# A row maximum over 64 MB: all loads but the first issued from GpSimd's queue in place of SP's

## The chip, the cores and the metric

The kernel runs on one core of a Trainium2 chip. The time is that of the device, in microseconds (us), for one execution of the whole program. A time called that of the kernel is the median of its runs; a profile is one execution of it, recorded by the hardware profiler, whose own time is given beside its span.

## The reference

```python
def setup_inputs():
    batch, seq, dim = 32, 512, 1024
    return {"x": np.random.randn(batch, seq, dim).astype(np.float32)}

def reference(x):
    return np.max(x, axis=-1).astype(np.float32)
```

There are 32 x 512 = 16384 rows of 1024 float32 values, 67.1 MB in all, and of each row the largest value is wanted: 16384 values, 64 KB. Each value of the input is read once and compared once.

## The kernel before, in words

The 16384 rows are spread over the 128 partitions of the on-chip memory, 128 rows for each partition. "A row" below means one row of 1024 values (4 KB) in every partition, that is 0.5 MB in all; the kernel handles 128 such rows.

The list `BLOCKS` fixes, ahead of time, how many rows each load brings. The first list has 15 loads, of 14, 13, 12, 11, 9, 8, 8, 7, 6, 5, 5, 4, 4, 3 and 3 rows (112 in all); the second has three loads of two rows and nine of one row (15), and then comes one last row that is loaded in two halves (lines 67 and 68). Each partition's rows of one list lie one behind the other in DRAM, so a load of n rows is, for each partition, one unbroken run of n x 4 KB.

The rows land in `ring`, a buffer with room for `RING = 45` rows per partition. A load takes the next free stretch of it, and goes back to its beginning where the stretch would run over the end (lines 54 and 55). So loads 1, 2 and 3 (14 + 13 + 12 = 39 rows) fit side by side; load 4 (11 rows) goes back to row 0, where load 1 lay; load 5 lies over what loads 1 and 2 held, load 6 over loads 2 and 3, loads 7 and 8 over load 3 and beyond, and so on.

One load (line 57) and one reduction on VectorE (line 58) make a step. The reduction reads all n rows of the load and writes n maxima per partition into `res`. The framework puts in the waits: a reduction waits until its load has landed; a load waits until the reductions that read the rows it overwrites are through; and a load also waits for the landing of the load eight before it, since there are eight completion semaphores that take turns. VectorE works in program order, and so does the queue of each engine that issues loads.

All 29 loads are issued from SP (SyncE), on its hardware queue. GpSimd (POOL) does nothing but four small MEMSETs of constants at the start, which the framework adds. TensorE has no work.

At the end, the last row's first half is reduced into the element of `tail` that lies just ahead of the second half (line 69), and the final reduction goes over that element and the second half together (line 70). Two stores are issued from ScalarE: that of the first 112 rows' maxima, held back until the last reduction of the loop (lines 73 and 74), and that of the other 16 (line 75).

Of the kernel before, what the change touches and what calls it, by code (L numbers as in the profile page):

```python
# [1 line left out]

# [4 lines left out]


F32 = mybir.dt.float32

BLOCKS = [
    [14, 13, 12, 11, 9, 8, 8, 7, 6, 5, 5, 4, 4, 3, 3],
    [2, 2, 2, 1, 1, 1, 1, 1, 1, 1, 1, 1],
]
RING = 45
SYNC = mybir.DependencyInfo(mybir.DependencyClass.Sync, mybir.DependencyReason.DATA)


@with_exitstack
def kernel(
    ctx: ExitStack,
    tc: tile.TileContext,
    x: bass.AP,
    out: bass.AP,
):
    nc = tc.nc
    P = 128
    X = mybir.AxisListType.X  # L30

    xf = x.flatten_outer_dims()
    N, D = xf.shape
    H = D // 2
    I = N // P
    of = out.flatten_outer_dims()

    once = ctx.enter_context(tc.tile_pool(name="once", bufs=1))
    ring = once.tile([P, RING, D], F32)
    res = once.tile([P, I], F32)  # L40

    PAD = 16
    tail = once.tile([P, PAD + H], F32)

    at = first = 0
    views = []
    for loads in BLOCKS:
        S = sum(loads) + (loads is BLOCKS[-1])
        xb = xf[first * P:(first + S) * P, :].rearrange("(p i) d -> p i d", p=P)
        dst = bass.AP(tensor=of.tensor, offset=of.offset + first * P, ap=[[S, P], [1, S]])  # L50
        views.append((dst, res[:, first:first + S]))
        b = 0
        for n in loads:
            if at + n > RING:
                at = 0
            xc = ring[:, at:at + n, :]
            nc.sync.dma_start(out=xc, in_=xb[:, b:b + n, :])  # L57
            reduce = nc.vector.reduce_max(out=res[:, first + b:first + b + n], in_=xc, axis=X)  # L58
            at += n
            b += n  # L60
        first += S
    assert first == I

    if at + 1 > RING:
        at = 0
    half = ring[:, at, :H]
    nc.sync.dma_start(out=half, in_=xb[:, b, :H])
    nc.sync.dma_start(out=tail[:, PAD:], in_=xb[:, b, H:])
    nc.vector.reduce_max(out=tail[:, PAD - 1:PAD], in_=half, axis=X)  # L69
    nc.vector.reduce_max(out=res[:, I - 1:], in_=tail[:, PAD - 1:], axis=X)  # L70


    store = nc.scalar.dma_start(out=views[0][0], in_=views[0][1])
    tc.add_manual_dep(store.ins, reduce.ins.name, SYNC, reason="behind the loads")
    nc.scalar.dma_start(out=views[1][0], in_=views[1][1])


# [1 line left out]
_INS = ['x']  # L79
_OUTS = [((32, 512), 'float32')]  # L80


# [23 lines left out]
```

## Time and profile before

| | before |
|---|---|
| median of the runs | 164.97 us (164.94 to 165.01, two runs) |
| the profiled execution | 165.17 us |
| its span, first to last instruction | 163.4 us |
| VectorE busy | 139.0 us, 29 instructions |
| GpSimd busy | 0.2 us, 4 instructions |
| read from DRAM | 67.11 MB, 411 GB/s over the span |
| the SP queue's packets, as a share of 16 DMA engines | 96.6% |

In the profile, DVE is VectorE, POOL is GpSimd, SP is SyncE; SPq is SP's queue with the loads that it issues. L57 is line 57 of the kernel. The page cuts the span into 40 slices and gives, for each, the busy share in tenths (9 is 90% or more). A group of instructions is shown as line, engine, operation, output<-input with their shapes, then the busy time and the mean of one in nanoseconds, and at the end how long the engine had been idle before them and what ended that idle time. A line of DMA issues ends with the size in KB and the time in microseconds from the issue to the landing. The timeline gives start, length, engine, line and operation; in brackets is the idle time before it and what ended it. The waits give engine, line, what was waited for, the total in microseconds, how many times, and the longest. The chain that ended last is followed back from the last instruction, at each step to what released it. A table by stretch of time gives the stretch, its length, VectorE's and GpSimd's busy time with the number of instructions, the granted TensorE clock, the DMA share and the GB/s.

### The profile page before, as it was taken

The page shows a single profiled execution, that of the slowest core. Times are in us where ns is not written, and L with a number is a line of the kernel's source. Part 1 is how long each engine was busy: PE and PEld are TensorE (multiplying, and loading weights), DVE is VectorE, ACT ScalarE, POOL GpSimd, SP SyncE. Part 2 cuts the span into 40 slices and gives each one's busy share as a digit, 9 for nine tenths or more (in the row PEclk, how much of TensorE's full clock was granted, in tenths as well). Part 3 has the DMA queues.
Part 4 walks back from the last instruction along what each step waited for, and adds up shares of the span by engine and source line. Part 5 has one row for each costly group of instructions (what it writes and reads, how often), then busy time and mean ns, then how long its engine had stood idle before and what let it go on. Part 6 is the DMA issues. An engine that isn't in the chain of part 4 may idle for free.

```text
span 163.4 us, 117 instructions
## 1 busy us (share of the span) xinstructions
DVE 139.0 (85%) x29; POOL 0.2 (0%) x4
## 2 busy tenths in 40 slices
DVE  0000099989998999999999999999999999999994
POOL 0000000000000000000000000000000000000000
DMA  6999999999989989999989999999999999999990
GB/s 225 449 449 449 433 417 417 417 401 529 433 385 430 452 386 432 433 433 441 457 385 481 401 442 422 409 438 421 446 409 425 437 410 422 427 407 409 409 355 16
DMA packets 4464, 67.18 MB, mean 411 GB/s; under 512 B 752, under 2 KB 752, under 8 KB 2160
## 3 DMA queue, kind: packets, MB, share of 16 engines
q1 hardware_dynamic: 4176, 67.11, 96.6%
q10 hardware_dynamic: 288, 0.07, 0.2%
HBM read 67.11 MB, written 0.07 MB: 411 GB/s over the span
## 4 chain that ended last, share of the span: by engine, by line
DVE 49%; DMA 48%; SPq 1%; issue 0%
DMA ring<-in_x_dram 48%; DVE res L58 48%; SPq L57 1%; DVE res L70 0%; DVE tail L69 0%
## 5 line engine op out<-in xcount | busy, mean ns | idle before, releaser
L58 DVE TENSOR_REDUCE res<-ring 128x1 f32<-128x1024 f32 (+12 forms) x27 | 137.7, 5165 | 22.1 <-DMA ring<-in_x_dram 22.1
L70 DVE TENSOR_REDUCE res<-tail 128x1 f32<-128x513 f32 x1 | 0.7, 686 | 0.0
L69 DVE TENSOR_REDUCE tail<-ring 128x1 f32<-128x512 f32 x1 | 0.7, 682 | 0.0
L90 POOL MEMSET const-bfloat16-1.0<- 128x1 bf16 x1 | 0.1, 102 | 0.0
L90 POOL MEMSET const-uint8-127<- 128x1 uint8 x1 | 0.1, 102 | 0.0
L90 POOL MEMSET const-float32-0.0<- 128x1 f32 x1 | 0.1, 99 | 0.2 <-issue 0.2
L90 POOL MEMSET const-float32-1.0<- 128x1 f32 x1 | 0.1, 99 | 0.0
## 6 DMA issues: line engine op xcount, KB each, us to landing
ring<-in_x_dram SPq DMA_DIRECT2D x2, 4096.0 KB, 25.6
ring<-in_x_dram SPq DMA_DIRECT2D x1, 7168.0 KB, 19.6
ring<-in_x_dram SPq DMA_DIRECT2D x1, 6656.0 KB, 34.9
ring<-in_x_dram SPq DMA_DIRECT2D x1, 6144.0 KB, 48.9
ring<-in_x_dram SPq DMA_DIRECT2D x1, 5632.0 KB, 28.5
ring<-in_x_dram SPq DMA_DIRECT2D x2, 2560.0 KB, 38.4
ring<-in_x_dram SPq DMA_DIRECT2D x1, 4608.0 KB, 24.7
ring<-in_x_dram SPq DMA_DIRECT2D x9, 512.0 KB, 13.8
```

Of the source, the lines that this page charges most:

```text
L57: nc.sync.dma_start(out=xc, in_=xb[:, b:b + n, :])
L58: reduce = nc.vector.reduce_max(out=res[:, first + b:first + b + n], in_=xc, axis=X)
L69: nc.vector.reduce_max(out=tail[:, PAD - 1:PAD], in_=half, axis=X)
L70: nc.vector.reduce_max(out=res[:, I - 1:], in_=tail[:, PAD - 1:], axis=X)
L90: nc = _bacc.Bacc("TRN2", target_bir_lowering=False, num_devices=1)
```

## The change

Load 1 (14 rows) is issued from SP as before. The other 26 loads of the loop and the two halves of the last row are issued from GpSimd, whose DMAs go through the software queue[...]. The sizes, the order, the ring, the reductions and the stores are the same.

```diff
@@ in the loop over loads
             xc = ring[:, at:at + n, :]
-            nc.sync.dma_start(out=xc, in_=xb[:, b:b + n, :])
+            queue = nc.gpsimd if first + b else nc.sync
+            queue.dma_start(out=xc, in_=xb[:, b:b + n, :])
             reduce = nc.vector.reduce_max(out=res[:, first + b:first + b + n], in_=xc, axis=X)
@@ the last row, in two halves
     half = ring[:, at, :H]
-    nc.sync.dma_start(out=half, in_=xb[:, b, :H])
-    nc.sync.dma_start(out=tail[:, PAD:], in_=xb[:, b, H:])
+    nc.gpsimd.dma_start(out=half, in_=xb[:, b, :H])
+    nc.gpsimd.dma_start(out=tail[:, PAD:], in_=xb[:, b, H:])
```

`first + b` is the number of rows loaded so far; it is zero for load 1 alone.

## The prediction

> **What bounds the kernel now.** I read the page first (parts 1 to 3), then the DMA issues with their landings, then the timeline of the first 64 us, then the waits, and last the chain of waits. From the page, busy time, queues and issues:
>
> ```profile
> DVE 139.0 (85%) x29; POOL 0.2 (0%) x4
> ...
> DVE  0000099989998999999999999999999999999994
> ...
> DMA  6999999999989989999989999999999999999990
> ...
> q1 hardware_dynamic: 4176, 67.11, 96.6%
> ...
> ring<-in_x_dram SPq DMA_DIRECT2D x1, 7168.0 KB, 19.6
> ring<-in_x_dram SPq DMA_DIRECT2D x1, 6656.0 KB, 34.9
> ring<-in_x_dram SPq DMA_DIRECT2D x1, 6144.0 KB, 48.9
> ```
>
> Two resources are nearly full at once. The DMA engines work from start to end (96.6%). VectorE (DVE) is idle for five slices and then full to the end. The 4176 packets of the SP queue are 29 loads of 144, that is 128 data packets (one for each partition's whole run) and 16 completions. So the first load, 14 rows of 4 KB per partition, is 128 packets of 56 KB, eight on each of the 16 engines. The last three lines are loads 1, 2 and 3, with time from issue to landing. The timeline shows how they were issued and what waited for them:
>
> ```profile
> 0.73 1.32 SPq L57 DMA_DIRECT2D ring<-in_x_dram  x3
> 20.31 15.09 DVE L58 TENSOR_REDUCE res<-ring 128x14 f32<-128x14336 f32 x1 [20.31 <-DMA ring<-in_x_dram]
> 35.43 0.33 SPq L57 DMA_DIRECT2D ring<-in_x_dram  x1
> 36.05 14.02 DVE L58 TENSOR_REDUCE res<-ring 128x13 f32<-128x13312 f32 x1 [0.65 <-DMA ring<-in_x_dram]
> 50.58 12.95 DVE L58 TENSOR_REDUCE res<-ring 128x12 f32<-128x12288 f32 x1 [0.51 <-DMA ring<-in_x_dram]
> ...
> 160.38 0.69 DVE L70 TENSOR_REDUCE res<-tail 128x1 f32<-128x513 f32 x1
> ```
>
> Three loads are issued together, within 1.3 us, and they arrive strictly one behind the other: at 20.3, 36.05 and 50.6 us. That is what one queue does: load 1 has all 16 engines to itself. Load 2 (6.816 MB) takes 15.74 us after load 1, or 433 GB/s; this is the full rate that I use below. At it load 1 alone (7.34 MB) is 16.95 us of moving, 2.12 us a packet on each engine, and a packet of load 2 (52 KB) is 15.74/8 = 1.97 us. The waits:
>
> ```profile
> DVE res L58 <- DMA ring<-in_x_dram: 22.1, 5, 20.3
> ...
> SPq L57 <- DVE res L58: 77.4, 7, 15.1
> SPq L57 <- DMA ring<-in_x_dram: 59.4, 13, 18.2
> ```
>
> This is the line that decides. Of VectorE's 22.1 us of waiting, 20.3 are for the very first load; after that only 1.8 us in four waits are left in 140.8 us. VectorE's own work, once begun, is therefore a second bound that lies only 1.8 us below the first. Any delay of the first landing beyond 1.8 us goes to the end of the kernel one for one. The chain of waits gives the same picture from the other side: 48.5% of it is loads and 48.0% reductions on line 58.
>
> **What the Trainium skill says.** (1) The page "DMA: Bandwidth & Descriptors", section "Queues, rings and completion order", says that each DMA engine goes round-robin between the queues that have work for it, a packet of one and then a packet of the next. The trace of before cannot confirm it, since only the SP queue carries loads. (2) The same page, "Issuing engines are not separate DMA queues", says that DMAs of different issuing engines run on the same 16 engines and interleave. (3) Its section "SWDGE vs HWDGE vs iDMA" gives the software queue's packets as preferably at most 4096 B and at most 64 descriptors; for a run of 52 KB that leaves open whether it is one packet or cut. (4) "SBUF — State Buffer", section "Who interferes with whom", says that a tensor reduce on this chip never contends with GpSimd for the SBUF port, so VectorE should not starve the software descriptor generation; nothing in the trace of before shows it.
>
> **The change, part by part.** The bytes, the 29 reductions, the ring of 45 rows and the two stores stay. What moves:
>
> *SP's waits move to POOL.* Twenty-eight issues, with their waits for reductions and for earlier landings, go from SP to POOL. Behind a waiting issue on POOL stand only later loads, as on SP now; POOL's own work is four MEMSETs of 0.1 us before the loads begin. No other engine waits for POOL. Cost of the move itself: nothing, as long as the software issue is hidden.
>
> *The software issue.* The trace of before has no software DMA. A hardware issue takes 0.33 to 0.44 us of SP; the skill gives about 1 us to the first byte for the software path against 0.6 (same DMA page, "Latency and other measured facts"), so per load between nothing and, doubling it for safety, 2 us. I take 1 us. Its cover is worked out below and is over 8 us; only where POOL needs more than about 1.28 us per issue in the run of one-row loads would it eat into that cover, slowly.
>
> *Load 1 stands alone on SP, and loads 2 and 3 start beside it.* This is the part that counts. Neither of loads 2 and 3 waits for anything, so POOL issues them at about 0.8 us, and their packets reach the engines about when load 1's do. By round-robin each engine then takes a packet of load 1, one of load 2, one of load 1. Load 1 has eight packets on each engine; between its first and its eighth stand seven of load 2, 7 x 1.97 = 13.8 us. Load 1 lands at 20.3 + 13.8 = 34.1 us. Load 2 lands two us later, at 36.1, no earlier than now, and VectorE has no use for it before load 1 in any case. Bounds: eight packets in front if POOL comes first (36.0 us); six if POOL's first packet comes some 4 us late or an engine has already taken up a second packet of load 1 (32.1 us). I take seven.
>
> *What VectorE does from there.* It starts at 34.1. Reduction 1 ends at 49.2, reduction 2 at 63.1, reduction 3 at 76.1. Is it ever starved again? Load 4 (11 rows, slots of load 1) is issued at 49.2; load 3 has emptied the engines at about 50.6, load 4 needs 5.77 MB / 433 = 13.3 us plus up to 2 for its start, and lands near 65; it is wanted at 76.1. Load 5 (9 rows, needs load 2's slots) is issued at 63.1, lands near 76, is wanted at 87.9. Loads 6, 7 and 8 need load 3's slots and are issued at 76.1; they land near 88, 98 and 106, wanted at 97, 106 and 115. From there on the engines run without a gap at the old pace and the last half row lands near 163, wanted at 172. So each load is 8 to 11 us early, VectorE works without a pause, and this is the cover that hides the software issues, the two or three DMA gaps of about 1 us after reductions 1 to 3, and a transfer rate up to about 7% lower over the last 113 us.
>
> *Sum.* 34.1 (start) + 139.0 (VectorE busy, page) = 173.1. In the profile of before the span ends 2.3 us after VectorE (163.4 against 160.38 + 0.69), for the last store and the closing waits: 175.4. The profiled execution took 165.17 us for a span of 163.4, 1.77 us around it: 177.2. The profiled execution lies 0.2 us above the median of the runs, 164.97, so **177.0** for a median. Put as a difference: 13.8 us of delay less the 1.8 us of idle time that vanishes, +12.0 us, 7.3%.
>
> **Rivals.**
>
> *R1, not slower: load 1 goes first after all.* If its eight packets are drained as one turn (one DMA is one packet for the arbiter), or if the software queue's first bytes come very late, loads 2 and 3 arrive behind it as now. VectorE starts at 20.3 and the time is 165 to 165.5. For it: load 1 is issued a little earlier than POOL can be heard, and the trace shows no case of two queues. Against: the two statements of the skill on interleaving, and one packet per partition in the page's counts. The point from which it decides: within 2% (3.3 us) the first landing may slip by 3.3 + 1.8 = 5.1 us, two packets of load 2 in front instead of seven; POOL's first byte would have to come later than about 12 us.
>
> *R2, the software queue cuts runs into small packets.* Eight turns of 4 KB cost load 1 almost nothing (8 x 1.97/13 = 1.2 us), but all later loads then move at the rate of short packets. The stretch from 140 to 150 us, where loads have one and two rows, moved 414 GB/s:
>
> ```profile
> 140.00:150.00 10.00, 10.00 (x5) 0.00 (x0) 1.00 1.01 414
> ```
>
> The 59.8 MB behind load 1 then take 144.4 us in place of 138.1, and a last stage 2 to 3% slower still is possible: +6 to +8 us, 171 to 173.
>
> *R3, the software queue keeps its turn for a whole DMA.* Then an engine takes one packet of load 1, all of load 2, one of load 1, all of load 3, and the other six. Load 1 lands when all three have, at 50.6 us; 50.6 + 139.0 + 2.3 + 1.8 = 193.7. Against it: packets preferably small.
>
> **How the numbers follow.** Forecast (5.5 to 8.5 packets in front, or a little end work on POOL) 0.70, own range 174.5 to 179.5; R1 0.13; R2 0.08; R3 0.06; the rest, 0.03, something slower still, or a gain that I see no source for, since VectorE's 139.0 us cannot begin before load 1's 17 us of moving. The range 169 to 181 holds the forecast and R2 and leaves R1 and R3 out, 0.19. A measurement of this kernel tells 2% from no change; faster by that 0.02, within it 0.14, slower 0.84.
>
> **What would show it.** In the page's DMA part a second queue with 28 x 144 = 4032 packets; more if runs are cut (R2). Load 1 from issue to landing about 33 us in place of 19.6, load 2 nearly as it was. VectorE idle for eight slices in place of five, then without a wait. VectorE's waits: one of about 34 us and nothing else. Busy time 139.0 as before. The DMA row with dips after 50, 65 and 76 us and an early end. The forecast is wrong if VectorE starts near 20 us (R1) or near 50 (R3), or if it starts at 34 and waits for loads later, which would mean a slow software path.

## The result, and the profile after

| | before | after |
|---|---|---|
| median of the runs | 164.97 us | 180.09 us (180.09 to 180.10, two runs) |
| ratio to before | | 1.092, 95% interval 1.089 to 1.094 |
| the profiled execution, its span | 165.17 us, 163.4 us | 180.09 us, 178.3 us |

The kernel is 15.1 us slower. From the page of the changed kernel, the lines that answer to those shown of before:

```profile
DVE 138.7 (78%) x29; POOL 15.0 (8%) x32
...
DVE  0000000099999999997999999999999999999994
...
DMA  6999999989870047989989999999999999999980
...
q0 software_dynamic: 3904, 59.77, 78.9%
q1 hardware_dynamic: 144, 7.34, 9.9%
...
ring<-in_x_dram SPq DMA_DIRECT2D x1, 7168.0 KB, 33.2
ring<-in_x_dram POOLq DMA_DIRECT2D x1, 6656.0 KB, 34.6
ring<-in_x_dram POOLq DMA_DIRECT2D x1, 6144.0 KB, 48.5
```

Load 1, 7168 KB, now takes 33.2 us from issue to landing, where it took 19.6. Loads 2 and 3 take what they took (34.9 and 48.9 before), although they come from the software queue, `q0 software_dynamic` on the page. VectorE is idle for eight slices and not five; then it is full, but for one slice with a 7. GpSimd's 15.0 us are, but for the four MEMSETs, the time of its 28 issues. The DMA row has a hole that the forecast did not have, slices 13 to 15. The waits of the changed kernel have this line for VectorE (total, times, longest):

```profile
DVE res L59 <- DMA ring<-in_x_dram: 37.2, 3, 35.9
```

And its timeline, first up to 100 us, of which the first issues are shown, then in stretches from 45 to 62, from 60 to 66 and from 74 to 82 us (PEq is TensorE's sequencer, which has no work here):

```profile
1.25 2.22 POOL L58 DMA_DIRECT2D ring<-in_x_dram  x4 [0.81 <-PEq L102]
3.47 0.54 POOL L69 DMA_DIRECT2D tail<-in_x_dram  x1
...
35.90 29.01 DVE L59 TENSOR_REDUCE res<-ring 128x13 f32<-128x13312 f32 x2 [35.90 <-DMA ring<-in_x_dram]
...
49.84 27.93 DVE L59 TENSOR_REDUCE res<-ring 128x14 f32<-128x14336 f32 x2
65.21 1.05 POOL L58 DMA_DIRECT2D ring<-in_x_dram  x2 [61.20 <-DVE res L59]
...
64.83 15.20 DVE L59 TENSOR_REDUCE res<-ring 128x12 f32<-128x12288 f32 x3
...
81.17 11.89 DVE L59 TENSOR_REDUCE res<-ring 128x11 f32<-128x11264 f32 x1 [1.14 <-DMA ring<-in_x_dram]
```

The first reduction is that of load 2 (13 rows), at 35.9 us; that of load 1 (14 rows) comes second, at 49.84. The compiled program has exchanged the two. It has also brought two one-row reductions forward, behind that of load 3 (the group x3 from 64.83). Their loads and that of the very last half row (L69) go out at the start, behind loads 2 and 3. POOL's next load, number 4, must wait for reduction 1, whose rows it overwrites, and goes out at 65.21 us, 61.2 us after POOL's last issue at the start. So VectorE waits for it once more, 1.14 us.

The sum closes: start 35.9, VectorE busy 138.7, its later waits 37.2 - 35.9 = 1.3, from VectorE's end to the span's end 2.3 (178.3 - 175.34 - 0.69): 178.2 us against the measured 178.3.

The packet records of the trace show what happened to load 1. These are the starts, in us, of the first to the eighth packet on a DMA engine (each time that of the earliest of the 16 engines; the others follow within 0.9 us):

```
before, load 1 (56 KB)   1.72  4.54  6.66  8.77 10.88 13.00 15.11 17.22   last one ends 19.95
after,  load 1 (56 KB)   1.74  4.54  8.62 12.70 16.78 20.85 24.93 29.01   last one ends 31.59
after,  load 2 (52 KB)   6.66 10.74 14.82 18.89 22.97 27.05 31.12 33.09   last one ends 35.52
```

After two packets of load 1 the queues alternate strictly, one packet each, until load 1 is done. Six packets of load 2 stand ahead of its last one. Yet it lands only at 0.74 + 33.2 = 33.9 us, 2.3 us after its last byte, where before it was 0.35. The completion is a packet too, one of 4 bytes on each engine, and it waits for one more packet of load 2 (31.12 to 33.09): the 16 completions of load 1 start from 33.09 to 33.55 us. That makes seven turns in all, the number of the forecast, but six of them ahead of the last data packet and one ahead of the completion.

### The profile page after: what moved, and what is told of

It reads as the page before. It is cut to its first block, busy times and chain, and to the rows that moved or that the text cites. A ratio compares the mean times of both kernels' runs of the same rounds, so it can differ in the third digit from the quotient of the medians.

```text
span 178.3 us, 115 instructions
## 1 busy us (share of the span) xinstructions
DVE 138.7 (78%) x29; POOL 15.0 (8%) x32
## 3 DMA queue, kind: packets, MB, share of 16 engines
q0 software_dynamic: 3904, 59.77, 78.9%
## 4 chain that ended last, share of the span: by engine, by line
DVE 60%; DMA 38%; issue 0%; POOL 0%; PEldq 0%
DVE res L59 59%; DMA ring<-in_x_dram 38%; DVE res L71 0%; DVE tail L70 0%; POOL ring L58 0%; PEldq L102 0%
## 5 line engine op out<-in xcount | busy, mean ns | idle before, releaser
L59 DVE TENSOR_REDUCE res<-ring 128x1 f32<-128x1024 f32 (+12 forms) x27 | 137.5, 5161 | 37.2 <-DMA ring<-in_x_dram 37.2
L58 POOL DMA_DIRECT2D ring<-in_x_dram x26 | 13.8, 533 | 147.7 <-DVE res L59 116.6
L68 POOL DMA_DIRECT2D ring<-in_x_dram x1 | 0.5, 541 | 2.2 <-DVE res L59 2.2
L69 POOL DMA_DIRECT2D tail<-in_x_dram x1 | 0.5, 541 | 0.0
## 6 DMA issues: line engine op xcount, KB each, us to landing
ring<-in_x_dram SPq DMA_DIRECT2D x1, 7168.0 KB, 33.2
```

Source lines behind the costliest of these rows:

```text
L58: queue.dma_start(out=xc, in_=xb[:, b:b + n, :])
L68: nc.gpsimd.dma_start(out=half, in_=xb[:, b, :H])
L69: nc.gpsimd.dma_start(out=tail[:, PAD:], in_=xb[:, b, H:])
```

## The experiments

Two theories stood against each other: A, that the loss comes from two queues that have work at once, at the start; B, that the software queue is slow. And the order of the instructions had to be told apart from both. The diffs below are against the changed kernel, that of the second run against the first. Where the order is held, the ties of the first run are in place too and are not shown again, and the two halves of the last row go by the queue of the late loads.

**The order of the source.** The changed kernel, with each load and each reduction tied to the one before it on its engine; the tie orders the instructions and adds no wait:

```diff
+    def pin(engine, made):
+        if engine in last:
+            tc.add_manual_dep(made.ins, last[engine].ins.name, ORDER, reason="program order")
+        last[engine] = made
+        return made
-            queue.dma_start(out=xc, in_=xb[:, b:b + n, :])
-            reduce = nc.vector.reduce_max(...)
+            pin(queue, queue.dma_start(out=xc, in_=xb[:, b:b + n, :]))
+            reduce = pin(nc.vector, nc.vector.reduce_max(...))
```

> The changed kernel with its loads and its reductions held in the order of the source (14, 13, 12, 11 rows and so on); the queues are those of the change. Theory A (two queues take turns packet by packet, so load 1 lands near 34 us, and the rest of the loss is the order: the compiled change reduces load 2 ahead of load 1 and brings two one-row loads forward): VectorE starts at 34 us with load 1 and never waits again; 177.0 us, about 3 us less than the change. Rival B (the software queue is slow by itself): the order is worth nothing, it stays at 180.

Measured: 176.45 us, 1.070 of before (1.068 to 1.071), 3.6 us less than the change. VectorE's line in the waits:

```profile
DVE res L68 <- DMA ring<-in_x_dram: 33.9, 1, 33.9
```

The timeline up to 100 us:

```profile
33.89 71.92 DVE L68 TENSOR_REDUCE res<-ring 128x14 f32<-128x14336 f32 x6 [33.89 <-DMA ring<-in_x_dram]
49.27 0.53 POOL L67 DMA_DIRECT2D ring<-in_x_dram  x1 [46.82 <-DVE res L68]
```

One wait in the whole kernel, 33.9 us, and load 4 issued at 49.27. This is the forecast's schedule. Its order is that of before, the queues are those of the change, and it still loses 11.5 us.

**Only the loads in order**, with the reductions left to the compiler (which exchanges the first two again, but brings none forward):

```diff
-            reduce = pin(nc.vector, nc.vector.reduce_max(...))
+            reduce = nc.vector.reduce_max(...)
```

> Queues as in the change; only the loads are held in the order of the source, while the reductions keep the order that the compiled change gives to its first ones (load 2 ahead of load 1, then load 3, load 4 and so on, with no one-row reductions brought forward). If the exchange of the first two reductions carries the rest of the loss: VectorE starts near 35.9 us with load 2, reduction 1 ends near 65, load 4 can be issued only then and lands near 81, while reduction 3 ends at 77.8, so VectorE waits some 3.4 us (in the change 2.4 us of that were filled by two one-row reductions): 181.5 to 182.5 us, slower than the change. If the loads brought forward (GpSimd's queue filled with small loads ahead of load 4) carried it: about 176.5 us, as with everything in order.

Measured: 182.36 us, 1.106 of before (1.104 to 1.107). The timeline up to 100 us:

```profile
35.94 41.87 DVE L68 TENSOR_REDUCE res<-ring 128x13 f32<-128x13312 f32 x3 [35.94 <-DMA ring<-in_x_dram]
65.24 1.04 POOL L67 DMA_DIRECT2D ring<-in_x_dram  x2 [62.80 <-DVE res L68]
...
81.27 21.55 DVE L68 TENSOR_REDUCE res<-ring 128x11 f32<-128x11264 f32 x2 [3.46 <-DMA ring<-in_x_dram]
```

That is 5.9 us more than with both held, and the order of the two runs differs in reductions 1 and 2 alone. So it is their exchange that costs, in two ways: VectorE starts 2.0 us later (35.9 against 33.9), and load 1's rows in the ring come free at 65 us and not at 49, which makes load 4 late. The loads and reductions brought forward are a help: they fill 2.3 of the 3.46 us. No run held the reductions alone.

**All loads on the software queue**, order held:

```diff
-            queue = nc.gpsimd if first + b else nc.sync
+            queue = nc.gpsimd
```

> As in the run with the order held, but load 1 too is issued from GpSimd, so only one queue carries loads. A: load 1 lands near 20.8 us (half a microsecond later than from SP, since GpSimd issues it at 1.25 us and not at 0.74), no turns are taken, 165 to 166 us, as before the change. B: at least 180, as every load now goes through software.

Measured: 165.87 us, 1.005 of before (1.004 to 1.007). The page has a single queue for the loads:

```profile
q0 software_dynamic: 4048, 67.11, 96.1%
```

The timeline has the first issues and the first three reductions:

```profile
1.24 1.72 POOL L67 DMA_DIRECT2D ring<-in_x_dram  x3 [0.80 <-PEq L111]
21.16 15.09 DVE L68 TENSOR_REDUCE res<-ring 128x14 f32<-128x14336 f32 x1 [21.16 <-DMA ring<-in_x_dram]
...
36.89 14.02 DVE L68 TENSOR_REDUCE res<-ring 128x13 f32<-128x13312 f32 x1 [0.64 <-DMA ring<-in_x_dram]
...
51.42 12.95 DVE L68 TENSOR_REDUCE res<-ring 128x12 f32<-128x12288 f32 x1 [0.51 <-DMA ring<-in_x_dram]
```

Everything goes through software and the kernel is 0.9 us slower than before. This is the timeline of before, 0.85 us late. B falls here. Of the 0.9 us, 0.5 is that POOL issues at 1.24 us where SP issued at 0.73, and 0.4 that the first packet comes 1.38 us after the issue (at 2.62) and not 0.99 (at 1.72).

**Two hardware queues**, load 1 from SP and the others from ScalarE, order held:

```diff
-            queue = nc.gpsimd if first + b else nc.sync
+            queue = nc.scalar if first + b else nc.sync
```

> Order held, load 1 from SP, all others from ScalarE's hardware queue; no software queue at all. A: hardware queues take the same turns, load 1 lands near 34 us, 176.5 to 177.5 us. B: about 165, as there is no software left.

Measured: 178.52 us, 1.082 of before (1.080 to 1.084). That is outside A's numbers by 1 us, and on the side away from B: there is no software left, and the loss is larger.

```profile
q10 hardware_dynamic: 4320, 59.84, 80.4%
q1 hardware_dynamic: 144, 7.34, 10.0%
```

That is the page; the timeline up to 100 us:

```profile
0.72 99.21 ACTq L67 DMA_DIRECT2D ring<-in_x_dram  x11
0.73 0.37 SPq L67 DMA_DIRECT2D ring<-in_x_dram  x1
35.76 71.92 DVE L68 TENSOR_REDUCE res<-ring 128x14 f32<-128x14336 f32 x6 [35.76 <-DMA ring<-in_x_dram]
```

ScalarE issues at 0.72 us, half a microsecond ahead of POOL, and load 2's first packet starts at 4.48 us in place of 6.49 with the order held: one turn more, eight of 1.97 us, which is 20.3 + 15.7 = 36.0 us against the measured 35.76. The prediction had eight turns as a bound; the expectation for this run left them out.

**Loads 1 to 3 on SP, the rest on the software queue**, order held:

```diff
-            queue = nc.gpsimd if first + b else nc.sync
+            queue = nc.gpsimd if first + b >= 39 else nc.sync
```

> Order held, loads 1, 2 and 3 from SP, loads 4 to 29 from GpSimd's software queue. Load 4 waits for reduction 1, so the two queues barely have work at once. A: load 1 lands near 20.3 us, 165 to 166 us. B: 26 of the 28 moved loads are still software, so most of the loss stays, 178 or more.

Measured: 174.03 us, 1.055 of before (1.053 to 1.057). Both expectations missed. The issues on its page, with the time to landing:

```profile
ring<-in_x_dram SPq DMA_DIRECT2D x1, 7168.0 KB, 19.2
ring<-in_x_dram SPq DMA_DIRECT2D x1, 6656.0 KB, 34.6
ring<-in_x_dram SPq DMA_DIRECT2D x1, 6144.0 KB, 58.6
```

Its timeline, with reductions 1 and 3 and the issue of load 4:

```profile
20.01 15.09 DVE L68 TENSOR_REDUCE res<-ring 128x14 f32<-128x14336 f32 x1 [20.01 <-DMA ring<-in_x_dram]
35.41 0.67 POOL L67 DMA_DIRECT2D ring<-in_x_dram  x1 [34.97 <-DVE res L68]
...
60.26 12.95 DVE L68 TENSOR_REDUCE res<-ring 128x12 f32<-128x12288 f32 x1 [10.50 <-DMA ring<-in_x_dram]
```

Load 1 lands at 20.0 us, as A has it, and the loss comes from A's mechanism at another place, which the expectation overlooked: load 4 is issued at 35.41 us, when load 3 has hardly begun (its first packet starts at 35.01). From the packet records, load 4 comes in after three of load 3's eight packets; the other five and the completion take turns with packets of 44 KB: 6 x 1.67 = 10.0 us. Load 3 lands 9.7 us late (60.24 against 50.5 in before), and the step waits 10.50 us for it.

**Small packets on the other side.** Loads 2 and 3 as two loads of every other row each, so that a packet is one row (4 KB), order held:

```diff
+            if n in (13, 12):
+                for odd in (0, 1):
+                    pin(queue, queue.dma_start(out=xc[:, odd::2, :], in_=xb[:, b + odd:b + n:2, :]))
+            else:
                 pin(queue, queue.dma_start(out=xc, in_=xb[:, b:b + n, :]))
```

> Order held, queues as in the change, but loads 2 and 3 are each issued as two loads of every other row, so that each of their packets is 4 KB and no longer 52 or 48 KB; load 1 keeps its 56 KB packets. Theory A1 (a turn is a packet, whatever its size): between load 1's packets stand seven or eight packets of 4 KB at about 0.16 us each, so load 1 lands near 21.5 us, not 34; loads 2 and 3 move some 6% slower in all, and the time is 166 to 168 us. Rival A2 (the two queues share the bytes evenly): load 1 lands near 34 us as with large packets, 177 us.

**Half the packet size.** Load 2 as one load of 7 rows and one of 6, order held:

```diff
-    [14, 13, 12, 11, ...
+    [14, 7, 6, 12, 11, ...
```

> Order held, queues as in the change, but load 2 of 13 rows is split into one of 7 and one of 6 rows, each with its own reduction. A1 (a turn is a packet): seven packets of 28 KB (1.06 us each) stand in front of load 1's landing, 20.3 + 7.4 = 27.7 us, and the kernel takes 27.7 + 139.2 + 4.1 = 171 us. A2 (even shares of bytes): load 1 lands near 34 us, 177 us.

Measured: 166.92 us (1.011 of before, 1.009 to 1.013) with small packets and 170.27 us (1.032, 1.030 to 1.033) with half. Load 1's issue line in each, small packets first:

```profile
ring<-in_x_dram SPq DMA_DIRECT2D x1, 7168.0 KB, 20.7
```

```profile
ring<-in_x_dram SPq DMA_DIRECT2D x1, 7168.0 KB, 26.9
```

A turn is a packet, whatever its size; the even share of bytes falls. The landing moves with the size of the other queue's packets alone: landed at 21.4 us with 4 KB (0.16 us a packet), 27.7 with 28 KB (1.06 us), 33.9 with 52 KB (1.97 us). Seven turns on 20.3 give 21.4, 27.7 and 34.1. The run with small packets loses 1.9 us and not only these 1.1, because VectorE then waits 0.9 us more for loads 2 and 3 than before.

**Load 2 waits for load 1's landing**, on the software queue, order held:

```diff
+            if first + b == 14:
+                tc.add_manual_dep(load.ins, load1.ins.name, SYNC, reason="load 1 alone")
```

> Order held, queues as in the change, but the first load on GpSimd (load 2) waits until load 1 has landed; so load 1 has the DMA engines to itself and the software queue carries the rest. Theory A: VectorE starts at 20.3 us; load 2's first packet goes out about 1.4 us after load 1 has landed, 21.7 us in place of 19.3, and as the loads bound the kernel this gap of 2.4 us comes out at the end: 167 to 168 us. If the software queue were the cause: 176 or more.

Measured: 168.34 us, 1.020 of before (1.019 to 1.022), 0.3 us above what A gave. The timeline up to 100 us:

```profile
20.31 15.09 DVE L72 TENSOR_REDUCE res<-ring 128x14 f32<-128x14336 f32 x1 [20.31 <-DMA ring<-in_x_dram]
20.59 1.20 POOL L67 DMA_DIRECT2D ring<-in_x_dram  x2 [20.14 <-DMA ring<-in_x_dram]
...
39.40 14.02 DVE L72 TENSOR_REDUCE res<-ring 128x13 f32<-128x13312 f32 x1 [4.01 <-DMA ring<-in_x_dram]
```

Load 1 is back at 20.31 us. Load 2 lands at 39.4 and not at 36.05, and these 3.35 us are the loss of 3.4. Its first packet starts 2.6 us later than in before (21.96 against 19.34), and 2.65 us pass to the start of its second where it is 1.97 between the later ones; this second part was not in the expectation. No version beat the kernel before.

## Why the prediction was right, and where it was off

The measured 180.09 us lie in the range of 169 to 181, but above the 174.5 to 179.5 that the prediction gave for its own case. 11.5 us of the 15.1 come from the mechanism that it forecast, at 12.0. The other 3.6 have a cause that no term of it stood for; that the wide range took them in was luck.

- *What bounds the kernel.* VectorE's 139 us behind load 1's landing, with 1.8 us of room. Right: in all runs in which VectorE waits for load 1 alone, the time is that landing plus 142.6 to 142.8 us (33.9 and 176.45; 35.8 and 178.52; 27.7 and 170.27).
- *Load 1 at 34.1 us by taking turns.* Right, at 33.9, though the count of seven is in part luck. The prediction had all seven ahead of the last data packet; there were six, its lower bound, and the completion, for which it had no turn, added the seventh. The statements of the Trainium skill on turns by packet and on interleaving ("DMA: Bandwidth & Descriptors", "Queues, rings and completion order" and "Issuing engines are not separate DMA queues") are borne out, with one packet of load 1 every 4.08 us in place of every 2.11, and the runs with smaller packets show that it is packets that take turns, not bytes. Why load 2's first packet came only after two of load 1 is open: POOL issued it at 1.25 us, and it started at 6.66, 5.4 us later, where with a single queue it was 1.38.
- *The step that failed: "It starts at 34.1. Reduction 1 ends at 49.2".* The forecast read the order of work from the source, and so do the sections on the kernel and on the change, which calls the order the same. For loads and reductions that don't depend on one another the compiled program need not keep it: reductions 1 and 2 were exchanged once their loads stood in different queues. Against the kernel with the order of the source this cost 3.6 us (180.09 - 176.45). By the trace it is 2.0 us of later start and 1.3 us of waiting later on (35.9, and 1.14 of the 1.3, in the lines of after), and 0.2 us of busy time. The kernel with the order of the source is what the sum of the prediction describes, and lies 0.55 us below its 177.0: 0.2 us of the start and 0.5 of VectorE's busy time, 138.5 us in the three runs with a single wait, less 0.2 by which a profile of before was longer than the median and this one is not. Why the compiler chose this order is open.
- *The software issue is hidden.* Right, and smaller than assumed: 0.53 us per issue, and the first packet comes 1.38 us after it where the hardware queue took 0.99, so 0.4 us more. The packet durations are the same, 1.06 us for 28 KB in either queue.
- *R1 (load 1 first after all) and R3 (a whole DMA as a turn)* fall by the packet records. *R2 (runs cut to 4 KB)* falls too. The count of 3904 packets is not the 4032 that the prediction named: software put the 256 runs of 2 KB of the two half rows into 128 packets of 4 KB, which accounts for the whole difference, and it left longer runs whole, up to the 56 KB of load 1 in the run with all loads in software. For the short runs that agrees with what the Trainium skill gives as the preferred packet, at most 4096 B ("DMA: Bandwidth & Descriptors", "SWDGE vs HWDGE vs iDMA"); the long ones lie far above it.
- *VectorE and GpSimd do not disturb each other.* So it looks here: the 12-row reduction took 12.94 us with two of POOL's issues beside it (65.21 to 66.26) and 12.95 before, the 9-row one 9.74 us with two beside it and without.
- *DMA dips after 50, 65 and 76 us and an early end.* Right for the most part in the order of the source: by the packet records of the run that holds it, the DMA engines stand idle for about 1 us near 50 and near 76 us, hardly near 65, and the loads end near 163. Wrong in the changed kernel, which has one hole from 53 to 66 us while load 4 waits for the exchanged reduction 1. It cost 1.14 us only, since VectorE had work until 80.

## What to carry to other kernels

If one load is awaited ahead of all others, keep everything that could run beside it in the same queue behind it, or make the other queue's packets small: in these runs a second queue took every second turn, and a turn is a packet, here one partition's unbroken run, up to 56 KB and 2.1 us. The delay of the awaited load was, in every such run and within 0.4 us, the number of its packets per DMA engine that were still to come when the other queue's first packet started, and one for its completion, times the other queue's packet time: 6 + 1 in the change, 7 + 1 with ScalarE's queue, 5 + 1 for load 3 in the run with three loads on SP. It counts in full where the consumer has no idle time left; here 1.8 us of idle time took up a part. And look at the compiled order before working out a schedule; moving loads between queues can change the order of instructions that nobody touched.

## What the runs showed of the hardware that was not expected

- The completion of a load takes a turn of its own. From the end of load 1's last data packet to its landing it took 0.35 us with one queue, and 0.55, 1.4 and 2.3 us beside packets of 4, 28 and 52 KB.
- The software queue joins short runs, two of 2 KB to a packet, where the hardware queue moved each by itself.
- The first packet after a time without loads is slow. After 2.0 us without any, in the run in which load 2 waits, the second packet started 2.65 us after the first, where it was 1.97 between the later ones; at the start of the kernel before, load 1's first packet took 2.8 us on average and the later ones 2.12.
